# Key words 64 bytes further on, another order of score groups, and two of head 0's steps on VectorE, in a sparse and sliding attention block

## The chip, the cores and the metric

The kernel runs on one core of one Trainium2 chip. The metric is the device time of one execution in microseconds (us), the median of several runs. The profile is of one further execution, taken by the hardware profiler.

## What is computed

One decoder block for 512 tokens of 2048 features, all in float32: a normalisation, a wide projection, two groups of attention heads, a gate on each head, the output projection, the residual sum and a last normalisation. The heads that the change touches are the eight of group A (128 features each, two key groups of four heads):

```python
h = _rmsnorm(x, norm_g[l])
proj = h @ w_in[l]
...
qa = _rope(_heads(qa, N_HEADS_A, HEAD_DIM_A)).reshape(B, S, N_KV_A, GROUP_A, HEAD_DIM_A)
kc = _compress(_rope(_heads(kca, N_KV_A, HEAD_DIM_A)), cmp_k_pos[l], cmp_k_w1[l], cmp_k_w2[l])
...
o_cmp, p_cmp = _compressed_attention(qa, kc, vc)
sel_idx = _select_blocks(p_cmp, S)
o_sel = _selected_attention(qa, _rope(_heads(ksa, N_KV_A, HEAD_DIM_A)), _heads(vsa, N_KV_A, HEAD_DIM_A), sel_idx)
o_win = _banded_attention(qa, _rope(_heads(kwa, N_KV_A, HEAD_DIM_A)), _heads(vwa, N_KV_A, HEAD_DIM_A), WIN_A)
...
o_a = gates[..., 0:1] * o_cmp + gates[..., 1:2] * o_sel + gates[..., 2:3] * o_win
y_a = o_a.reshape(B, S, WIDTH_A) * jax.nn.silu(za)
```

With 512 tokens there are 8 blocks to select from and 16 may be taken, and the window is 512, so both `o_sel` and `o_win` are causal attention over all earlier keys, with keys and values of their own. A head of group A is three softmaxes: over 31 compressed keys and over two full sets of keys.

## The kernel before, in words

**Two words for each number.** [...] To keep float32 precision each operand is split into a high word (a rounded copy, made by ScalarE) and a low word (the rest, a subtraction on VectorE), and each product is three matmuls: high by high, low by high, high by low. `mm3` (L118 to L121) does so for the projections. The splits of the weights are L542 (ScalarE, `whi`) and L543 (VectorE, `wlo`).

**Stages.** In order of time: the norm and the first projections, the eight heads of group B with their projections, the keys and values of group A, the eight heads of group A, the output projection. In the stage of group A's heads `pair(h)` projects the query and the gate of head h by `seven`, a scheme of seven half products of 24 matmuls each, 256 columns wide (named "22", "p", "21", "12", "u", "w", "q" after their operands, written to the banks `pj`). The query comes out in the tile `t` (the buffer "t1", of which there is one: the next head's query can't be begun, L608, before the last reader of this one's is done). `q_done` then rotates it: `turn` (L658 to L666) makes two products with the sine on VectorE (L661) and one with the cosine (L662), and adds them (L664); `q_split` (L257 to L262) makes the high word `qh` on ScalarE (L260) and the low word `ql` by a subtraction (L261). For heads 0 to 5 the sum L664 and the subtraction L261 are on GpSimd, for heads 6 and 7 on VectorE. After the last half product VectorE scales the gate (L677), and ScalarE (L681) and VectorE (L682) make its silu.

**The scores.** `attn_a(h)` takes the four query tiles of 128 tokens in two pairs. The keys lie in two tiles, `KH` (high words) and `KL` (low words), 32 compressed keys first and then 1024 columns in which the two full sets alternate by 128. They are filled for the first key group from L885 on and in `key_words` (L755 on), and after head 3 again, by DMA, with the second group's words (L1027): it is the same two tiles for all eight heads. The score matmuls (L932) put a query tile against the part of the keys that it can see, in groups of columns, each group in one bank of PSUM: one of 288 columns for query tile 0; 288 and 256 for tile 1; 288 and 512 for tile 2; 288, 512 and 256 for tile 3. Every group is done for the three word pairs (`qh` with `KH`, `qh` with `KL`, `ql` with `KH`), so a head has 24 score matmuls and the stage 192. VectorE then takes the minimum with the mask (L934, L938), ScalarE the exponentials (L944, L948) and the scaling (L959), TensorE transposes (L969, L981, L983), and the values follow (L975 to L977, L990, L992).

**What sets the order.** The program is written head after head, but a scheduler puts the instructions of each engine in a fixed order of its own, by a simulated timeline, before anything runs. It mixes the next head's half products between the scores, transposes and value products of the present one. Each engine then works through its list strictly in order. A change of one instruction's engine or shape can so move many others.

**Places of the operands.** The kernel gives its tiles places in steps of 64 bytes: `MOVING, EVEN, STILL, BELOW = 0, 16, 32, 48` are places of weight words in units of 4 bytes, and some tiles are longer than their use (`K` has 32 spare columns). In the program's memory map `KH` and `KL` begin 64 bytes past a multiple of 128 bytes, as `xh` does, whose columns move through TensorE in the half products; `qh` and `ql`, and the weight words that stand still in the half products of this stage, begin at a multiple of 128.

Of the kernel before, what the change touches and what calls it, by code (L numbers as in the profile page):

```python
# [11 lines left out]
F32R = mybir.dt.float32r  # L12
# [5 lines left out]
P = 128  # L18
# [9 lines left out]
CMP = 32  # L28
# [7 lines left out]
def hybrid_block(ctx, tc, xT, xtm, w0, wv0, wv1, wz, wq, wo0, wos, cw1, cw2, cpos, e2, rope, tabs, sinks, gT, fg, out):  # L36
    nc = tc.nc
    pe, act, dve, pool = nc.tensor, nc.scalar, nc.vector, nc.gpsimd

    def sb(name, bufs=1, side=None):  # L40
        return tc.tile_pool(name=name, bufs=bufs, side=side)
# [215 lines left out]
    def q_split(t1, engine=pool):  # L257
        qh = wk.tile([P, S], F32R, name="qh", tag="qh", bufs=1)
        ql = wk.tile([P, S], F32R, name="ql", tag="ql", bufs=1)
        last["qh"] = act.activation(qh, t1, AF.Copy).ins  # L260
        engine.tensor_tensor(out=ql, in0=t1, in1=qh.bitcast(F32), op=ALU.subtract)  # L261
        return qh, ql  # L262
# [231 lines left out]
    kv = kvstack.enter_context(sb("kvA", side="right"))  # L494
# [5 lines left out]
    KH = KL = None  # L500
# [157 lines left out]
    def turn(v, out=None, engine=None):  # L658
        t2 = wk.tile([P, S], F32, name="t2", tag="t2", bufs=1)
        for a, b in ((0, 64), (64, 0)):  # L660
            dve.tensor_tensor(out=t2[a:a + 64], in0=v[b:b + 64], in1=sinA[b:b + 64], op=ALU.mult)  # L661
        dve.tensor_tensor(out=v, in0=v, in1=cosA, op=ALU.mult)  # L662
        if out is None:
            last["turn"] = (engine or dve).tensor_tensor(out=v, in0=v, in1=t2, op=ALU.add).ins  # L664
        else:
            dve.tensor_tensor(out=out, in0=by_block(v), in1=by_block(t2), op=ALU.add)  # L666

    def by_block(v):
        return v.rearrange("p (b j) -> p j b", j=16)

    def pair(h, hooks=None, extra=None):
        def q_done(qv):
            turn(qv, engine=pool if h < 6 else dve)
            return q_split(qv, pool if h < 6 else dve)

        qq, zr = seven(2 + h, done=q_done, hooks=hooks, extra=extra, final=h == 7)
        last["jj"] = dve.tensor_tensor(out=zr, in0=zr, in1=rstdb, op=ALU.mult).ins  # L677

        def silu():
            st = wk.tile([P, S], F32, name="st", tag="st")  # L680
            act.activation(st, zr, AF.Tanh, scale=0.5)  # L681
            dve.scalar_tensor_tensor(out=st, in0=st, scalar=1.0, in1=zr, op0=ALU.add, op1=ALU.mult)  # L682
            return st

        return qq, silu if h == 7 else silu()
# [198 lines left out]
                     "12": [lambda: compressed_values(*hidden)]}, early)  # L884
    ahead.close()  # L885
    kv = kvstack.enter_context(sb("kvK", side="right"))
    KH, KL = [kv.tile([P, CMP + 1056], F32R, name=f"K{e}")[:, 0:CMP + 1024] for e in "HL"]
    for e, k in enumerate((KH, KL)):
        act.activation(k[:, 0:CMP], k0w[:, e].bitcast(F32), AF.Copy)
    sum_of_head = fifth(0)  # L890
# [18 lines left out]
    def attn_a(h, qh, ql, st):  # L909
# [4 lines left out]
        for pair in range(2):  # L914
# [5 lines left out]
            for i in range(2):  # L920
                qt = 2 * pair + i
                n = (qt + 1) * P
                sp = pss.tile([P, 1536], F32, name="sp", tag="sp")
                groups = [(224, 512, 0)]
                if qt >= 1:
                    groups.append((512, 768 if qt == 1 else 1024, 288))
                if qt == 3:
                    groups.append((1024, 1280, 800))
                qs = slice(qt * P, (qt + 1) * P)
                for pi, (qq, kk) in enumerate(((qh, KH), (qh, KL), (ql, KH))):  # L930
                    for (a, b, ko) in groups:
                        pe.matmul(sp[:, a:b], qq[:, qs], kk[:, ko:ko + b - a], start=pi == 0, stop=pi == 2)  # L932
                blk = sp[:, 256:256 + 2 * n].rearrange("p (t w c) -> p w t c", w=2, c=P)
                dve.tensor_tensor_reduce(out=tc_[:, qt, :], in0=sp[:, 224:256], in1=cmask[:, qt * CMP:(qt + 1) * CMP],  # L934
                                         scale=-SCALE_A, scalar=1e38, op0=ALU.add, op1=ALU.min, accum_out=mn[:, i, 0:1])
                for w in range(2):
                    tv = tt[:, off:off + n]
                    last["score", qt] = dve.tensor_tensor_reduce(  # L938
                        out=tv.rearrange("p (t c) -> p t c", c=P), in0=blk[:, w],
                        in1=dmask[:, 512 - n:512].rearrange("p (t c) -> p t c", c=P),  # L940
                        scale=-SCALE_A, scalar=1e38, op0=ALU.add, op1=ALU.min, accum_out=mn[:, i, 1 + w:2 + w]).ins
                    views.append((i, w, tv))
                    off += n
                act.activation(tc_[:, qt, :], tc_[:, qt, :], AF.Exp, bias=mn[:, i, 0:1], scale=-1.0,  # L944
                               accum_out=dn[:, i, 0:1])
                for w in range(2):
                    tv = views[2 * i + w][2]
                    last["exp", qt] = act.activation(tv, tv, AF.Exp, bias=mn[:, i, 1 + w:2 + w], scale=-1.0,  # L948
                                                     accum_out=dn[:, i, 1 + w:2 + w]).ins
# [58 lines left out]
    for h in range(8):  # L1008
        qq, st = pair(h) if h else head0
        if h == 7:  # L1010
            def behind(f, *a):
                with tc.issue_after(last["dma"]):
                    return f(*a)

            first_units = [load_raw(wo0[:, 0, 0])]
            behind(words_back, range(4))
            first_units.append(behind(load_raw, wo0[:, 0, 1]))
            for j in range(4, 8):
                y_back(j)
            behind(words_back, range(4, 6))  # L1020
            first_units.append(behind(load_raw, wo0[:, 0, 2]))
            for j in range(4):
                behind(y_back, j)
        attn_a(h, *qq, st)
        if h == 3:
            for e in range(2):
                nc.sync.dma_start((KH, KL)[e].bitcast(F32), Kd[e])  # L1027
            for kt in range(NQ - 1):
                for e in range(2):
                    nc.sync.dma_start((VH, VL)[e][:, kt].bitcast(F32), Vd[e, :, kt])  # L1030
# [120 lines left out]
    for c, u, ms in ((0, 0, ()), (0, 1, ()), (0, 2, ()), (1, 0, (0, 1, 2)), (1, 1, (3, 4)), (1, 2, (5, 6)), (0, 3, ()),  # L1151
# [4 lines left out]
        with tc.issue_after(recent["mm"]) if (c, u) == (1, 3) else nullcontext():  # L1156
            for j in range(4):
                f = ORDER[4 * u + j]
# [361 lines left out]
```

## Time and profile before

| | us |
|---|---|
| median of 3 runs | 804.39 |
| lowest and highest run | 802.62, 804.96 |
| the profiled execution's own time | 802.8 |
| its span in the profile | 801.0 |

The span is the time from the first to the last instruction; 1.8 us of the profiled execution's time lie outside it. In the profile PE is TensorE (PEld its weight loads), DVE VectorE, ACT ScalarE, POOL GpSimd and SP the queue that issues most DMAs. Consecutive matmuls overlap in the records: each is shown with about 0.28 us, but the next one begins after 0.11 us, so what a matmul costs is read from start to start and not from its own duration. The same holds in part for the other engines, whose next instruction begins a little before the end of the last. The granted clock of TensorE was 0.997 of full speed over the execution. The stage of group A's heads is the stretch from 416 us to 650 us.

### The profile page before, as it was taken

Reading aid. Unit: us, or ns where it says so; the run is one execution under the profiler, and the core shown is the slowest. Engines: PE = TensorE matmul, PEld = TensorE weight load, DVE = VectorE, ACT = ScalarE, POOL = GpSimd, SP = SyncE. Lnnn points to the kernel's source line nnn. Section 1 sums busy time; section 2 is a strip of 40 time slices with the busy share of each in tenths; the row PEclk is TensorE's granted clock in tenths of the full one; section 3 lists DMA queues with packets and bytes.
Section 4 is the critical chain, followed back from the end, with each engine's and each line's share of the span. In section 5 each row is a group of like instructions: output and inputs, shape, how many; then the busy total and the mean of one; then the engine's idle time right before and its main releaser. Section 6 shows DMA issues by size and latency. Waiting matters only on the chain.

```text
span 801.0 us, 15316 instructions
## 1 busy us (share of the span) xinstructions
PE 789.6 (99%) x5693; PEld 739.1 (92%) x5693; DVE 686.3 (86%) x1407; ACT 504.7 (63%) x1103; POOL 108.3 (14%) x111
## 2 busy tenths in 40 slices
PE   9999999999999999999999999999999999999996
PEld 8788888888888899999999999999999999999996
DVE  7668988889989597759999999998999798978895
ACT  6646657655666356664447778777777867553545
POOL 3615002110121000323210110110100000000000
PEclk9999999999999999999999999999999999999998
DMA  7572243564373469887723213225216836797845
GB/s 239 172 242 81 79 144 106 171 171 150 101 210 106 158 200 281 257 269 194 207 82 106 68 53 119 82 92 159 71 50 216 296 120 219 257 266 193 258 86 211
DMA packets 49563, 131.05 MB, mean 164 GB/s; under 512 B 6000, under 2 KB 8848, under 8 KB 49488
## 3 DMA queue, kind: packets, MB, share of 16 engines
q1 hardware_dynamic: 43376, 110.89, 42.3%
q0 software_dynamic: 5824, 18.65, 10.5%
q8 instruction: 45, 0.74, 0.4%
q10 hardware_dynamic: 288, 0.52, 0.2%
q14 instruction: 30, 0.25, 0.1%
HBM read 113.23 MB, written 16.81 MB: 162 GB/s over the span
## 4 chain that ended last, share of the span: by engine, by line
PE 86%; DVE 6%; DMA 3%; ACT 2%; issue 2%; POOL 0%; SPq 0%; DVEq 0%; ACTq 0%
PE pj L119 16%; PE pj L121 15%; PE pj L120 15%; PE oa L120 5%; PE oa L119 5%; PE oa L121 5%; PE sp L932 4%; PE bank L121 2%; PE bank L120 2%; PE bank L119 2%; DMA xr<-xT 2%; DVE wlo L543 2%; PE tp L969 2%; PE tp L384 2%; DMA raw<-wq 1%
## 5 line engine op out<-in xcount | busy, mean ns | idle before, releaser
L119 PE MATMUL pj<-xh,whi 128*128 128x256 f32 (+1 forms) x592 | 196.9, 333 | 0.6 <-ACT t L608 0.5
L121 PE MATMUL pj<-xh,wlo 128*128 128x256 f32 (+1 forms) x592 | 196.2, 331 | 0.0
L120 PE MATMUL pj<-xl,whi 128*128 128x256 f32 (+1 forms) x592 | 196.1, 331 | 0.0
L119 PEld LDWEIGHTS pj<-xh,whi 128*128 128x128 f32 x592 | 111.4, 188 | 11.0 <-ACT t L608 0.9
L121 PEld LDWEIGHTS pj<-xh,wlo 128*128 128x128 f32 x592 | 111.4, 188 | 10.1
L120 PEld LDWEIGHTS pj<-xl,whi 128*128 128x128 f32 x592 | 111.4, 188 | 9.7
L543 DVE TENSOR_TENSOR wlo<-raw,whi 128x1024 fp32r<-128x1024 f32 (+2 forms) x80 | 92.9, 1172 | 7.8 <-ACT whi L542 7.2
L542 ACT ACTIVATE whi<-raw 128x1024 fp32r<-128x1024 f32 (+2 forms) x80 | 77.6, 985 | 30.7 <-DVE raw L581 11.5
L99 DVE TENSOR_TENSOR wlo<-raw,whi 128x1024 fp32r<-128x1024 f32 (+1 forms) x61 | 72.1, 1184 | 22.8 <-ACT whi L97 22.3
L97 ACT ACTIVATE whi<-raw 128x1024 fp32r<-128x1024 f32 (+1 forms) x60 | 56.6, 945 | 28.8 <-PE pj L120 14.8
L120 PE MATMUL oa<-wlo,xh 128*128 128x256 f32 x200 | 55.5, 278 | 0.0
L119 PE MATMUL oa<-whi,xh 128*128 128x256 f32 x200 | 55.4, 278 | 0.0
L121 PE MATMUL oa<-whi,xl 128*128 128x256 f32 x200 | 55.2, 276 | 0.0
L121 PE MATMUL pj<-pu,wlo 128*128 128x256 f32 x160 | 45.0, 281 | 0.5 <-DVE wlo L543 0.5
L119 PE MATMUL pj<-pu,whi 128*128 128x256 f32 x160 | 45.1, 282 | 0.4 <-DVE zr L581 0.4
L120 PE MATMUL pj<-pu,whi 128*128 128x256 f32 x160 | 44.7, 279 | 0.0
L289 DVE TENSOR_TENSOR pl<-tp,ph 128x512 fp32r<-128x512 f32 (+1 forms) x64 | 40.7, 651 | 3.1 <-ACT ph L288 2.9
L288 ACT ACTIVATE ph<-tp 128x512 fp32r<-128x512 f32 (+1 forms) x64 | 34.1, 560 | 9.6 <-PE tp L969 4.4
L363 ACT ACTIVATE ttb<-ttb,sums 128x256 f32<-128x256 f32 (+1 forms) x64 | 30.0, 471 | 14.4 <-DVE sums L356 14.4
L121 PEld LDWEIGHTS oa<-whi,xl 128*128 128x128 f32 x200 | 37.6, 188 | 0.0
L120 PEld LDWEIGHTS oa<-wlo,xh 128*128 128x128 f32 x200 | 37.6, 188 | 0.0
L119 PEld LDWEIGHTS oa<-whi,xh 128*128 128x128 f32 x200 | 37.5, 188 | 0.0
(401 smaller groups left out, 2369.8 us busy)
## 6 DMA issues: line engine op xcount, KB each, us to landing
raw<-wq SPq DMA_DIRECT2D x41, 512.0 KB, 4.4
raw<-wz SPq DMA_DIRECT2D x36, 512.0 KB, 4.0
cw<-cw SPq DMA_DIRECT2D x32, 256.0 KB, 4.0
raw<-wos SPq DMA_DIRECT2D x14, 512.0 KB, 5.9
rw<-wos SPq DMA_DIRECT2D x10, 512.0 KB, 4.8
xr<-xT SPq DMA_DIRECT2D x16, 256.0 KB, 3.4
rows<-xT SPq DMA_DIRECT2D x8, 512.0 KB, 4.7
raw<-wo SPq DMA_DIRECT2D x8, 512.0 KB, 6.0
```

The lines of the kernel that those rows point to most:

```text
L97: last["hi"] = act.activation(hi[:, :width], rw[:, :width], AF.Copy).ins
L99: last["lo"] = dve.tensor_tensor(out=lo[:, :width], in0=rw[:, :width], in1=hi[:, :width].bitcast(F32), op=ALU.subtract).ins
L119: pe.matmul(ps, ah, bh, start=first, stop=False, skip_group_check=go_on)
L120: pe.matmul(ps, ah, bl, start=False, stop=False, skip_group_check=go_on)
L121: recent["mm"] = pe.matmul(ps, al, bh, start=False, stop=last, skip_group_check=go_on).ins
L288: act.activation(ph, tp, AF.Copy)
L289: dve.tensor_tensor(out=pl, in0=tp, in1=ph.bitcast(F32), op=ALU.subtract)
L363: act.activation(tv, tv, AF.Exp, bias=mn[:, e, v:v + 1], scale=-1.0, accum_out=dn[:, e, v:v + 1])
L384: pe.transpose(tp[:, o:o + P], tts[kt + s][:, v, c0:c0 + P], ident)
L542: split_hi = act.activation(hi, src, AF.Copy).ins
L543: last["lo"] = dve.tensor_tensor(out=lo, in0=src, in1=hi.bitcast(F32), op=ALU.subtract).ins
L932: pe.matmul(sp[:, a:b], qq[:, qs], kk[:, ko:ko + b - a], start=pi == 0, stop=pi == 2)
```

## The change

Three edits. The two key tiles begin 16 columns (64 bytes) further on inside their buffers, which have the room, so nothing else moves in memory; both key groups lie in them. In query tile 3 of every head the group of 256 columns comes second and the group of 512 last. For head 0 the sum L664 and the subtraction L261 are on VectorE, as they were for heads 6 and 7; the sum of heads 1 to 5 stays on GpSimd.

```diff
     def pair(h, hooks=None, extra=None):
         def q_done(qv):
-            turn(qv, engine=pool if h < 6 else dve)
-            return q_split(qv, pool if h < 6 else dve)
+            turn(qv, engine=pool if 0 < h < 6 else dve)
+            return q_split(qv, pool if 0 < h < 6 else dve)
...
-    KH, KL = [kv.tile([P, CMP + 1056], F32R, name=f"K{e}")[:, 0:CMP + 1024] for e in "HL"]
+    KH, KL = [kv.tile([P, CMP + 1056], F32R, name=f"K{e}")[:, 16:CMP + 1040] for e in "HL"]
...
                 if qt == 3:
-                    groups.append((1024, 1280, 800))
+                    groups.insert(1, (1024, 1280, 800))
```

The scheduler's order of the instructions changes with it. VectorE's list at the end of head 0's projection, before against now; `t_4493` is head 0's query, `zr` its gate, and `raw` the weights of head 1:

```order
 L581 TENSOR_TENSOR zr<-zr,pj 128x256
 L543 TENSOR_TENSOR wlo<-raw,whi 128x1024
+L664 TENSOR_TENSOR t_4493<-t_4493,t_4689 128x512
 L677 TENSOR_TENSOR zr<-zr,rstdb 128x512
 L581 TENSOR_TENSOR raw<-raw 128x1024
+L261 TENSOR_TENSOR ql<-t_4493,qh 128x512
 L682 SCALAR_TENSOR_TENSOR st<-st,zr 128x512
 L581 TENSOR_TENSOR raw<-raw 128x1024
```

The sum and the low words, which GpSimd did beside this list, now stand in it: the sum behind a weight split, the low words behind the scaling of the gate and a sum of weights. GpSimd has nothing left to do in head 0. ScalarE's list at this place stays as it was: L260, L681, L608.

TensorE's list at query tile 3 of head 0, before against now:

```order
+L119 MATMUL pj<-xh,whi 128x256
+L120 MATMUL pj<-xl,whi 128x256
+L121 MATMUL pj<-xh,wlo 128x256
 L932 MATMUL sp<-KH,qh 128x288
+L932 MATMUL sp<-KH,qh 128x256
 L932 MATMUL sp<-KH,qh 128x512
-L932 MATMUL sp<-KH,qh 128x256
 L932 MATMUL sp<-KL,qh 128x288
+L932 MATMUL sp<-KL,qh 128x256
 L932 MATMUL sp<-KL,qh 128x512
-L932 MATMUL sp<-KL,qh 128x256
```

The nine score matmuls now end with one of 512 columns, and the tile comes three half-product matmuls later. From here to the end of the stage the lists differ in many places: which half-product matmuls stand between which scores, transposes and value products.

## The prediction on record

> **What bounds the kernel now.** I read the page first, then who TensorE waited for, then the stage of group A's heads (416 to 650 us) instruction by instruction. The page's busy times, then the waits of TensorE:
>
> ```profile
> PE 789.6 (99%) x5693; PEld 739.1 (92%) x5693; DVE 686.3 (86%) x1407; ACT 504.7 (63%) x1103; POOL 108.3 (14%) x111
> ...
> PE 86%; DVE 6%; DMA 3%; ACT 2%; issue 2%; POOL 0%; SPq 0%; DVEq 0%; ACTq 0%
> ```
>
> ```profile
> PE bank L176 <- DVE still L173: 1.2, 1, 1.2
> ...
> PE pj L119 <- ACT t L608: 0.5, 1, 0.5
> ...
> PE sp L932 <- DVE sums L938: 0.2, 1, 0.2
> ```
>
> TensorE sets the time: it is busy 99% of the span and makes 86% of the chain that ended last. In the stage of the heads the view of waits names two, 0.5 and 0.2 us. So there are two ways to gain here: to remove such a wait, or to bring the matmuls closer together.
>
> The change touches both. First the wait of 0.5 us, which lies at the end of head 0's projection. The engines' timelines there, GpSimd, VectorE, ScalarE, TensorE (start, duration, engine, line; in brackets the idle time and what ended it):
>
> ```profile
> 416.61 1.28 POOL L664 TENSOR_TENSOR t<-t,t 128x512 f32<-128x512 f32 x1 [21.54 <-DVE t L662]
> 418.64 1.49 POOL L261 TENSOR_TENSOR ql<-t,qh 128x512 fp32r<-128x512 f32 x1 [0.75 <-ACT qh L260]
> ```
>
> ```profile
> 414.63 1.23 DVE L543 TENSOR_TENSOR wlo<-raw,whi 128x1024 fp32r<-128x1024 f32 x1
> 415.77 0.69 DVE L662 TENSOR_TENSOR t<-t,cosA 128x512 f32<-128x512 f32 x1
> 416.37 0.42 DVE L581 TENSOR_TENSOR zr<-zr,pj 128x256 f32<-128x256 f32 x1
> 416.70 2.27 DVE L543 TENSOR_TENSOR wlo<-raw,whi 128x1024 fp32r<-128x1024 f32 x1
> 418.90 1.78 DVE L677 TENSOR_TENSOR zr<-zr,rstdb 128x512 f32<-128x512 f32 x1
> 420.60 1.21 DVE L581 TENSOR_TENSOR raw<-raw 128x1024 f32<-128x1024 f32 x1
> 421.73 0.68 DVE L682 SCALAR_TENSOR_TENSOR st<-st,zr 128x512 f32<-128x512 f32 x1
> ```
>
> ```profile
> 417.93 0.64 ACT L260 ACTIVATE qh<-t 128x512 fp32r<-128x512 f32 x1 [1.63 <-POOL t L664]
> 420.71 0.63 ACT L681 ACTIVATE st<-zr 128x512 f32<-128x512 f32 x1 [2.15 <-DVE zr L677]
> 421.25 0.36 ACT L608 ACTIVATE t<-pj 128x256 f32<-128x256 f32 x1
> ```
>
> ```profile
> 420.47 0.28 PE L121 MATMUL pj<-pu,wlo 128*128 128x256 f32 x1
> 420.59 0.29 PE L932 MATMUL sp<-KH,qh 128*128 128x288 f32 x1
> 420.71 0.30 PE L932 MATMUL sp<-KL,qh 128*128 128x288 f32 x1
> 420.85 0.29 PE L932 MATMUL sp<-KH,ql 128*128 128x288 f32 x1
> 421.66 0.39 PE L119 MATMUL pj<-xh,whi 128*128 128x256 f32 x1 [0.52 <-ACT t L608]
> 421.88 0.28 PE L120 MATMUL pj<-xl,whi 128*128 128x256 f32 x1
> ```
>
> While GpSimd runs, VectorE's split takes 2.27 us against 1.23 for the same shape just before, and its scaling L677 takes 1.78 against 0.69 for another product of that shape (L662). VectorE so comes 2.1 us late, ScalarE waits 2.15 us for L677, its copy L608 runs at 421.25, and TensorE, which wants to go on at about 420.98 (0.13 after its third score matmul), begins at 421.66: 0.7 us lost.
>
> Second, the pace of the matmuls. Stretches of half products, first and last start, from the timeline of TensorE:
>
> ```profile
> 415.83 0.28 PE L119 MATMUL pj<-xh,whi 128*128 128x256 f32 x1
> ...
> 424.71 0.28 PE L120 MATMUL pj<-xl,whi 128*128 128x256 f32 x1
> ...
> 428.22 0.52 PE L932 MATMUL sp<-KH,qh 128*128 128x288 f32 x2
> ...
> 429.30 0.28 PE L119 MATMUL pj<-pu,whi 128*128 128x256 f32 x1
> ...
> 434.29 0.28 PE L121 MATMUL pj<-xh,wlo 128*128 128x256 f32 x1
> 434.40 0.64 PE L932 MATMUL sp<-KH,qh 128*128 128x288 f32 x3
> ...
> 435.84 0.28 PE L119 MATMUL pj<-xh,whi 128*128 128x256 f32 x1
> ...
> 437.95 0.28 PE L119 MATMUL pj<-qw,whi 128*128 128x256 f32 x1
> ```
>
> From 415.83 to 420.47 lie 41 steps, 113 ns each. From 421.88 to 424.71, right behind query tile 0's scores, 24 steps take 118 ns each, with the same engine clock and shape. From 429.30 to 434.29, behind tile 2's scores (which end with 512 columns), 44 steps take 113 ns again; from 435.84 to 437.95, behind tile 3's nine (which end with 256), 18 steps take 117 ns. So TensorE has two paces, 4.6 ns apart, it keeps one for a whole stretch, and the scores between switch it. What switches it the trace doesn't say; that operands' places have a part in it is a surmise from the fact that engine, shape and clock are the same.
>
> **The change part by part.** *Head 0 on VectorE.* Removed from GpSimd: 1.28 and 1.49 us; added to VectorE, priced by the two heads where it does them now:
>
> ```profile
> L261 DVE TENSOR_TENSOR ql<-t,qh 128x512 fp32r<-128x512 f32 x2 | 1.4, 688 | 0.0
> ...
> L664 DVE TENSOR_TENSOR t<-t,t 128x512 f32<-128x512 f32 x2 | 1.4, 684 | 0.0
> ```
>
> 0.69 us each, about 0.60 from start to start (L662 to the next). With GpSimd silent I lay VectorE's new list out with its undisturbed steps: split 416.70, next start 1.14 later (as from 414.63 to 415.77), sum L664 at 417.84, scaling L677 at 418.44, weights L581 at 419.04, low words L261 at 420.18, done at 420.9. ScalarE: `qh` at 418.55, silu L681 at 419.2, both early. But L608 overwrites head 0's query, which L261 still reads. The view of tile `ql` lists ScalarE's L608 among those who waited for it:
>
> ```profile
> ACT t L608: 4.6, 4
> ```
>
> So L608 starts at about 420.95 instead of 421.25 and ends at 421.3; TensorE goes on at 421.35 instead of 421.66. The third score, at 420.85, needs `ql` too and comes some 0.1 us later, inside the same wait. Gain 0.3 us, not 0.7: the weights' sum L581, 1.2 us in front of L261, eats the rest. Bounds: 0.7 if it slides behind or the copy isn't held, nothing if the first weights arrive later than I think. Behind it stand L682 and a second L581; they start some 0.8 us earlier than before, which nobody on TensorE is shown to want.
>
> *The score matmuls themselves.* The view by source line counts them:
>
> ```profile
> L932 PE MATMUL sp<-KH,qh x64: 276/296/398, 420.6 to 637.1; 128*128 128x288 f32 x32, 128*128 128x256 f32 x16, 128*128 128x512 f32 x16
> ```
>
> 64 of each of three word pairs, 192. No run shows the new place of the keys under these operands. The nearest price is the difference of the two paces: 4.6 ns x 192 = 0.9 us, a gain or a loss. The nearest row for operands that both begin at the same place in 128 bytes is in an earlier stage (there 64 bytes past it, both), 512 columns:
>
> ```profile
> 77.24 0.39 PE L119 MATMUL opb<-xh,whi 128*128 128x512 f32 x1
> ...
> 80.64 0.39 PE L119 MATMUL opb<-xh,whi 128*128 128x512 f32 x1
> ```
>
> 15 steps, 226.7 ns each. The tile that starts at 428.22 (above) has three pairs of 288 and 512 columns in 1.08 us (to 429.30), 360 a pair; with 227 for the wide one, 133 are left for 288 columns, more than the 127.5 that 113.3 x 288/256 gives. I take a gain of 0.3 us.
>
> *Tile 3's new order.* It now ends with 512 columns, as tile 2 does, behind which the trace shows the quick pace. The slow stretch behind tile 3 costs 18 x 4 ns = 0.08 us; eight heads, 0.6 us. I take 0.5, since the key words moved as well and tile 2's pattern may not hold; bounds 0.6 and 0.
>
> *The stretches behind the other 24 tiles* change by the keys' place and by the new mixture. A stretch like that behind tile 0 (24 steps) costs 24 x 4.6 = 0.11 us when it is slow. If half are slow now, the two ends are 1.3 us of gain and of loss. I take a gain of 0.2: the place now equals that of `qh` and `ql`, as in the quick stage above, but the half products around keep theirs.
>
> The scheduler's other moves I cost at nothing: TensorE's list is full, and DVE's added 1.4 us lie in a stage where it has
>
> ```profile
> 416.00:650.00 234.00, 233.27 (x1959) 230.47 (x1959) 217.37 (x476) 180.36 (x446) 19.07 (x12) 1.00 0.36 119
> ```
>
> 16.6 of 234 us free (third busy time) and take 2.1 us of blocking away. If that cover fails, a late weight split costs TensorE about the 0.2 to 0.5 us of the two waits above, so 1 us either way goes into the range.
>
> Sum: 0.3 + 0.3 + 0.5 + 0.2 = 1.3 us of gain. Against the profiled execution's own time, 802.8 us, that gives 801.5. This execution stands 1.6 us under the median of the runs, 804.39; carried over, 803.1. About 0.3% (2.4 us) is what a measurement of this kernel can tell from no change: faster means under 802.0, slower over 806.8.
>
> **The rivals.** *The quick pace wins almost everywhere.* The scores gain 0.8, tile 3's stretches 0.6, the others 1.3, the wait goes whole, 0.7: together 3.4 us, 801.0. For it: 113 ns is the pace of most stretches above, and one switch sets a whole stretch. Against it: slow stretches begin after tile 0's scores too, where no order changes.
>
> *The place of the key words has no effect.* Then tile 3's order has none either, since there is no reason left why its end should matter, and only the 0.3 us at head 0 stay: 804.1. For it: that the two paces come from places is surmise. Against it: the pace follows what stood before, with all else equal. [...]
>
> *The slow pace wins: slower.* The new place makes the scores leave TensorE at 118 ns. Price: 0.9 us in the scores, less 0.3 at head 0, and 4.6 ns for every half-product matmul that turns from quick to slow. The same stage's row for the half products alone counts them:
>
> ```profile
> 416.00:650.00 234.00, 169.32 (x1314) 159.05 (x1313) 12.50 (x30) 7.83 (x21) 1.00 0.36 119
> ```
>
> 1314. From 390 of them on (1.8 us) it is over 0.3%; half of them, 657, cost 3.0 us, with the rest 3.6: 808.0. For it: behind tile 3, the state already lasted until the transposes. Against it: it must hit three in ten of all, and the end with 512 columns speaks for the other pace.
>
> *The edits don't do what they say:* the queue order shows both moved steps, and the new place holds for all heads, so this has no chance of its own.
>
> **How the numbers follow.** Forecast as summed 0.48 (its own range 801.3 to 805.0), quick pace 0.28, no effect of places 0.12, slow pace 0.12. Faster by over 0.3%: the quick pace and 0.05 of the forecast's edge, 0.33. Slower: 0.12. Within: 0.43 + 0.12 = 0.55. The range goes from 800.2 (the quick pace with most of the 1 us of the scheduler) to 805.8 (no effect, with the same the other way), and leaves out most of the slow case and the tails, about 0.2.
>
> **What the profile of the changed kernel would show.** No GpSimd work in head 0; VectorE's split at 1.23 us and L677 at 0.69 there; L608 right behind L261; the wait of TensorE for L608 at 0.2 us or gone. Behind tile 3's scores 113 ns from start to start in most heads. Pairs of 288 and 512 columns under 0.36 us. Wrong would be: `pj` stretches at 118 ns behind most tiles, a wait of TensorE for `wlo` or `ql` that isn't there now, or a stage whose length differs from 234 us by another amount than these terms.

## The result and the profile after

| | kernel before | changed kernel |
|---|---|---|
| median of the runs, us | 804.38 (802.62 to 804.96, 4 runs) | 813.23 (811.47 to 814.65, 4 runs) |
| ratio, with its 95% interval | | 1.0113 (1.0086 to 1.0139) |
| the profiled execution, us | 802.8 | 814.65 |
| its span, us | 801.0 | 812.9 |

The change makes the kernel 8.9 us slower; the interval of the ratio says 7 to 11 us. The forecast of 803.1 and its range up to 805.8 are both missed. The page of the changed kernel, busy times and chain:

```profile
PE 795.9 (98%) x5693; PEld 742.6 (91%) x5693; DVE 685.8 (84%) x1409; ACT 504.6 (62%) x1103; POOL 105.5 (13%) x109
...
PE 71%; DVE 13%; ACT 6%; DMA 6%; issue 3%; SPq 0%; POOL 0%; ACTq 0%; DVEq 0%
```

VectorE works no longer than before. TensorE's busy time grows by 6.3 us for the same 5693 matmuls: each is shown with about 0.28 us while the next begins after 0.11, so a delay shorter than the difference counts as busy. The chain moves as well. TensorE makes 71% of it and no longer 86%; VectorE has 13% and not 6%, ScalarE 6% and not 2%, DMA 6% and not 3%. The end is now set by handovers between engines. Who TensorE waited for (sum in us, times, longest):

```profile
PE pj L121 <- DVE wlo L543: 2.0, 5, 0.8
PE pj L119 <- ACT whi L542: 1.6, 2, 0.8
...
PE pj L119 <- ACT xh L1047: 1.1, 1, 1.1
PE sp L932 <- DVE sums L938: 1.0, 2, 0.8
PE oa L120 <- DVE wlo L1052: 0.7, 1, 0.7
...
PE sp L932 <- POOL ql L261: 0.3, 1, 0.3
...
PE op L976 <- DVE pl L289: 0.2, 1, 0.2
```

These seven rows are 6.9 us. Of these 4.4 lie in the heads' stage, where the view of before had 0.7, and 1.8 behind it. The other 0.7 lie ahead of it: of the five waits for L543 only two, 1.3 us, are in the stage; three are earlier, where the kernel before has two as well, of 0.5 us. None of the rows is at head 0. In the stage they are weight splits (L542, L543), softmax sums (L938) and low words (L261 on GpSimd, for head 1, and L289); behind the heads, the splits of the output projection (L1047, L1052). The stage of the heads in one row, to be held against the one the prediction quotes:

```profile
416.00:650.00 234.00, 229.44 (x1886) 224.74 (x1885) 206.75 (x457) 172.18 (x428) 16.14 (x10) 0.99 0.34 113
```

TensorE did 1886 matmuls until 650 us and not 1959, and VectorE, which was given work, was busy 206.75 us and not 217.37. Nobody is overloaded: all do less in the same time, because they wait for each other.

To see where time is lost I counted, for two traces, when TensorE had begun the same number of columns; the difference is the lag of the one behind the other. The lag of the changed kernel behind the kernel before, by the time of the latter:

| at, us | 400 | 430 | 450 | 500 | 520 | 580 | 600 | 640 | 650 | 680 | 700 |
|---|---|---|---|---|---|---|---|---|---|---|---|
| lag, us | -0.1 | -0.4 | 0.7 | 1.4 | 3.3 | 3.3 | 6.6 | 8.0 | 8.1 | 10.3 | 11.5 |

At head 0 the changed kernel is ahead. Then it falls back in steps near 446, 455, 516, 600, 638, 680 and 694 us of its own time, and from 700 us on nothing changes. The step at 516 us on ScalarE, VectorE and TensorE:

```profile
509.32 0.71 ACT L948 ACTIVATE tt<-tt,sums 128x512 f32<-128x512 f32 x1
509.93 0.19 ACT L948 ACTIVATION_READ_ACCUMULATOR tt<-tt,sums 128x1 f32 x1
513.10 0.69 ACT L957 ACTIVATE pc<-tc__5546,sums 128x128 f32<-128x128 f32 x2 [2.98 <-DVE sums L952]
513.70 2.34 ACT L959 ACTIVATE tt<-tt,sums 128x384 f32<-128x384 f32 x4
515.94 0.36 ACT L619 ACTIVATE zr<-pj 128x256 f32<-128x256 f32 x1
516.20 1.99 ACT L542 ACTIVATE whi<-raw 128x1024 fp32r<-128x1024 f32 x2
```

```profile
509.14 1.23 DVE L543 TENSOR_TENSOR wlo<-raw,whi 128x1024 fp32r<-128x1024 f32 x1
510.40 0.42 DVE L581 TENSOR_TENSOR t<-t,pj 128x256 f32<-128x256 f32 x1
510.74 0.69 DVE L682 SCALAR_TENSOR_TENSOR st<-st,zr 128x512 f32<-128x512 f32 x1
511.34 1.22 DVE L581 TENSOR_TENSOR raw<-raw 128x1024 f32<-128x1024 f32 x1
512.48 0.16 DVE L950 TENSOR_SCALAR sums<-sums 128x6 f32<-128x6 f32 x1
...
512.89 0.17 DVE L952 TENSOR_TENSOR sums<-sums,gates 128x6 f32<-128x6 f32 x1
```

```profile
517.30 0.38 PE L119 MATMUL pj<-pu,whi 128*128 128x256 f32 x1 [0.78 <-ACT whi L542]
```

ScalarE is done with the exponentials at 510.1 us and then stands still for 2.98 us: the next step in its list, L957, needs the normalisers L950 to L952, and VectorE's list has four larger steps in front of these. The copy L619 and the weight split L542 stand behind L957 and L959. By the program the copy has to wait for L682, which reads the gate that it overwrites (until 511.43 us), and for the half product that it copies (its last matmul is shown from 511.33 to 511.61 us), and the split for the weights that L581 makes (until 512.56 us). So for the last 1.5 us of the idle time the copy could run, and the split, which begins at 516.20, comes 3.6 us after its weights are there; TensorE waits for it. ScalarE takes its list strictly in order here: 1.5 us idle with a step ready behind the waiting one.

The largest step, 3.5 us near 600 us, has two parts. TensorE's waits there, and then two stretches of the view by windows (TensorE's granted clock is the third number from the end):

```profile
600.81 0.38 PE L119 MATMUL pj<-xh,whi 128*128 128x256 f32 x1 [0.79 <-ACT whi L542]
...
602.07 0.45 PE L121 MATMUL pj<-xh,wlo 128*128 128x256 f32 x1 [0.76 <-DVE wlo L543]
```

```profile
602.00:605.60 3.60, 3.53 (x17) 3.53 (x18) 1.68 (x8) 3.60 (x11) 0.00 (x0) 0.53 0.02 5
605.80:612.00 6.20, 6.20 (x50) 5.95 (x49) 4.77 (x13) 4.14 (x12) 0.00 (x0) 1.00 0.02 6
```

Two waits for splits stand close together, and right behind them the granted clock is about half for 3.4 us: 16 steps take 213 ns each and not 113, which is 1.6 us. In e2 (below), which is as slow, the clock is 1.00 over the whole stage, and behind a wait of 0.76 us for the same split the steps take 120 ns, so the slow clock adds to the loss of this execution and isn't what makes it. The profiled execution, 814.65 us, is the slowest of the four; whether the others have this stretch isn't known.

### The profile page after: what moved, and what is told of

It is laid out like the page before. It is cut to its first block, busy times and chain, and to the rows that moved or that the text cites. A ratio compares the mean times of both kernels' runs of the same rounds, so it can differ in the third digit from the quotient of the medians.

```text
span 812.9 us, 15329 instructions
## 1 busy us (share of the span) xinstructions
PE 795.9 (98%) x5693; PEld 742.6 (91%) x5693; DVE 685.8 (84%) x1409; ACT 504.6 (62%) x1103; POOL 105.5 (13%) x109
## 3 DMA queue, kind: packets, MB, share of 16 engines
q0 software_dynamic: 5824, 18.65, 10.6%
## 4 chain that ended last, share of the span: by engine, by line
PE 71%; DVE 13%; ACT 6%; DMA 6%; issue 3%; SPq 0%; POOL 0%; ACTq 0%; DVEq 0%
PE pj L121 13%; PE pj L119 13%; PE pj L120 13%; PE oa L120 4%; PE oa L121 4%; PE oa L119 4%; DVE wlo L543 4%; PE bank L121 2%; PE bank L120 2%; PE bank L119 2%; DMA xr<-xT 2%; PE sp L932 2%; DVE raw L581 2%; PE tp L384 2%; ACT whi L542 1%
## 5 line engine op out<-in xcount | busy, mean ns | idle before, releaser
L543 DVE TENSOR_TENSOR wlo<-raw,whi 128x1024 fp32r<-128x1024 f32 (+2 forms) x80 | 91.0, 1150 | 11.0 <-ACT whi L542 9.4
L542 ACT ACTIVATE whi<-raw 128x1024 fp32r<-128x1024 f32 (+2 forms) x80 | 77.3, 983 | 24.7 <-DVE raw L581 9.3
L289 DVE TENSOR_TENSOR pl<-tp,ph 128x512 fp32r<-128x512 f32 (+1 forms) x64 | 40.6, 650 | 3.0 <-ACT ph L288 2.8
```

The source lines that it names most:

```text
L289: dve.tensor_tensor(out=pl, in0=tp, in1=ph.bitcast(F32), op=ALU.subtract)
L542: split_hi = act.activation(hi, src, AF.Copy).ins
L543: last["lo"] = dve.tensor_tensor(out=lo, in0=src, in1=hi.bitcast(F32), op=ALU.subtract).ins
```

## The experiments

The theories named in the first four expectations: A, the scheduler's new lists of the engines cost the time; B, the new place of the key words brings the slow pace of the matmuls; C, the two steps on VectorE cost it themselves. All ratios are against runs of the kernel before, measured beside them on the same chip.

To hold lists, some kernels tie each instruction to the one ahead of it in a given list of its engine, without any semaphore, ahead of the scheduling:

```diff
         hybrid_block(tc, *args, out)
+        _keep_lists(tc, nc)
...
+            if before is not None:
+                tc.add_manual_dep(i, before.name, info, reason="list")
```

### Which part costs the time

**e1: the words alone.** Only this edit; the scheduler writes the same lists as before.

```diff
-    KH, KL = [kv.tile([P, CMP + 1056], F32R, name=f"K{e}")[:, 0:CMP + 1024] for e in "HL"]
+    KH, KL = [kv.tile([P, CMP + 1056], F32R, name=f"K{e}")[:, 16:CMP + 1040] for e in "HL"]
```

> Only the key words begin 64 bytes further on; every engine's list stays that of before. Theory A (the new lists of the engines cost the time): 803 to 805 us, at most 1.5 us off before, since 192 score matmuls at 4.6 ns are 0.9 us. Theory B (the new place puts TensorE in the slow pace): 807 to 813. Theory C (the two steps cost time by being on VectorE): 803 to 805.

803.59 us, ratio 1.0002 (0.9988 to 1.0016). Tile 2 of head 0 and the matmul behind it in this trace:

```profile
428.59 0.52 PE L932 MATMUL sp<-KH,qh 128*128 128x288 f32 x2
...
429.68 0.28 PE L119 MATMUL pj<-pu,whi 128*128 128x256 f32 x1
```

Three pairs of 288 and 512 columns take 1.09 us, 363 ns each; they took 360 before. The place of the keys doesn't change the time, and B falls.

It does change the pace of some stretches, both ways. Behind tile 3 of head 0, 18 steps of half products take 113 ns each here, and behind that of head 1, 13 steps; the scores have their old order, and the kernel before takes 117 and 118 there. The stage has 55 stretches of eight or more half products that can be compared in six traces. In nine of them the three traces with the old place (before, e3, e7) agree on the pace, the three with the new place (e1, e5, e6) agree too, and the two differ: six stretches, 131 steps, turn quick, and three, 59 steps, turn slow. At 4 to 5 ns a step, the net is an estimated 0.3 us.

**e2: head 0 on VectorE alone**, with the lists that the scheduler then makes.

```diff
-            turn(qv, engine=pool if h < 6 else dve)
-            return q_split(qv, pool if h < 6 else dve)
+            turn(qv, engine=pool if 0 < h < 6 else dve)
+            return q_split(qv, pool if 0 < h < 6 else dve)
```

> Only head 0's sum and low words go to VectorE, with the lists that the scheduler then makes; the scores and key words stay. Theory A (lists): 810 to 815 us, nearly all of the loss. Theory B (place of the words): 803 to 805. Theory C (the work on VectorE itself): 810 to 815.

813.44 us, ratio 1.0129 (1.0105 to 1.0154): the whole loss of the change. It is in this edit or in what the scheduler makes of it.

**e3: the same edit, the lists of the kernel before held**, the two steps put where the scheduler has them on VectorE.

> Head 0's sum and low words on VectorE, but every engine's list pinned to that of before; the two instructions stand in VectorE's list where the changed kernel has them, behind the weight split and behind the first sum of weights. Theory A (lists): 803 to 805 us, 0.3 under before by the sum made for head 0. Theory B (place): 803 to 805. Theory C (the work on VectorE itself): 810 to 815.

802.81 us, ratio 0.9988 (0.9977 to 0.9999): 1.0 us faster than before, and not slower. (The same program, measured again as e7, gives 0.9996.) Head 0 on VectorE, ScalarE and TensorE:

```profile
417.79 0.68 DVE L664 TENSOR_TENSOR t<-t,t 128x512 f32<-128x512 f32 x1
418.39 0.68 DVE L677 TENSOR_TENSOR zr<-zr,rstdb 128x512 f32<-128x512 f32 x1
418.99 1.22 DVE L581 TENSOR_TENSOR raw<-raw 128x1024 f32<-128x1024 f32 x1
420.12 0.68 DVE L261 TENSOR_TENSOR ql<-t,qh 128x512 fp32r<-128x512 f32 x1
```

```profile
420.90 0.38 ACT L608 ACTIVATE t<-pj 128x256 f32<-128x256 f32 x1 [1.16 <-DVE ql L261]
```

```profile
421.34 0.39 PE L119 MATMUL pj<-xh,whi 128*128 128x256 f32 x1
```

This is the layout of the prediction to within 0.06 us at each step. C falls.

**e4: GpSimd as before, but the lists of e2 held** for all other instructions.

> The code of before with both steps on GpSimd, but every engine's list pinned to the one that the scheduler made for head 0 on VectorE (the lists of e2_dve). Theory A (lists): 810 to 815 us, as slow as e2_dve though nothing moved to VectorE. Theory B (place): 803 to 805. Theory C (the work on VectorE itself): 803 to 805.

813.26 us, ratio 1.0117 (1.0098 to 1.0135). Without any of the three edits the new lists alone cost 9.5 us. A holds: two steps of 0.7 us moved, and the lists that the scheduler wrote around them cost all of it.

**e5: all three edits, the lists of before held**, and **e6**, the same with the low words ahead of the sum of weights in VectorE's list:

```diff
 L664 t<-t,t
 L677 zr<-zr,rstdb
+L261 ql<-t,qh
 L581 raw<-raw
-L261 ql<-t,qh
```

> All three edits (key words 64 bytes on, tile 3's groups in the new order, head 0's sum and low words on VectorE), with each engine's list of the kernel before held; the two moved steps stand on VectorE where the changed kernel has them, and only the groups of tile 3 change places. Theory A (the new lists of the engines cost the time): about 802.3 us, against 803.8 for the kernel before: the 1.0 us that head 0 alone gave with the old lists, and 0.5 for tile 3. Rival B' (the two placement edits cost something once they stand together, which neither the words alone nor VectorE alone showed): 804 or more. Either way no wait of TensorE for whi or wlo in the heads' stage.

> As e5, and one step more: on VectorE head 0's low words L261 stand ahead of the weights' sum L581 (1.2 us) instead of behind it. If the prediction's reading is right that this sum eats the rest of head 0's wait, L608 starts as soon as its product is there, at about 420.8 us, and TensorE goes on at 421.2 or before, 0.15 us or more sooner than in e3 (421.34). If the sum's lateness is what counts instead (the weights L581 feed a split that TensorE needs next), TensorE goes on no sooner, or loses about 0.5 us at the next weights. In the total the difference to e5 is under 0.5 us and inside the interval: the trace decides.

e5: 802.1 us, ratio 0.9985 (0.9972 to 0.9998); e6: 802.15 us, 0.9983 (0.9968 to 0.9998). Both beat the kernel before, e5 by 1.2 us with an interval from 0.2 to 2.2, and the changed kernel by some 10 us (1.0113 less 0.9985 of 803.3). The stage of the heads in e5, and the nine scores of tile 3 of head 1 with the half products behind them:

```profile
416.00:650.00 234.00, 233.79 (x1968) 231.32 (x1967) 217.09 (x480) 180.72 (x447) 16.32 (x10) 1.00 0.36 119
```

```profile
462.34 0.63 PE L932 MATMUL sp<-KH,ql 128*128 128x288 f32 x3
462.81 0.28 PE L120 MATMUL pj<-xl,whi 128*128 128x256 f32 x1
...
464.29 0.28 PE L121 MATMUL pj<-xh,wlo 128*128 128x256 f32 x1
```

1968 matmuls until 650 us. Behind tile 3, which now ends with 512 columns, 13 steps take 113.8 ns each, where before they took 118. But e1 takes 113 here with the scores in their old order: what goes with the quick pace at this place is the new place of the words, and not the order. Behind tile 3 of head 5 it goes with the order: 118 ns in before, e3, e7 and e1, 113 in e5 and e6. In e6 TensorE goes on 0.13 us after the third score, so without a wait, but it does so in e5 too, where VectorE happened to run 0.4 us further ahead of TensorE than in e3. That the sum of weights is what holds the rest of head 0's wait is therefore not shown; one execution's lead of VectorE is worth as much. e7, whose program is that of e3, goes on 0.14 us after its third score, and e3 0.48.

### Are other lists better

**e10: only the sum L664 on VectorE; e11: only the low words L261.** Each with the lists that the scheduler makes for it.

```diff
-            turn(qv, engine=pool if h < 6 else dve)
+            turn(qv, engine=pool if 0 < h < 6 else dve)
```

```diff
-            return q_split(qv, pool if h < 6 else dve)
+            return q_split(qv, pool if 0 < h < 6 else dve)
```

> Only head 0's sum of rotation products L664 on VectorE, the low words L261 still on GpSimd; the engines' lists as the scheduler draws them for this program. Theory S (any move between engines makes the scheduler draw other lists for the heads' stage, and their quality is a matter of luck): slower by some us or not, between 801 and 815, with waits of TensorE for whi or wlo wherever it is slower. Rival (it is the low words' move that spoils the lists): 803 to 804.

> Only head 0's low words L261 on VectorE, the sum L664 still on GpSimd; lists as drawn for this program. Theory S: anything between 801 and 815, with waits of TensorE for whi or wlo where it is slower. Rival (the sum's move spoils the lists): 803 to 804.

808.78 us, ratio 1.0055 (1.0033 to 1.0078), and 810.32 us, 1.0082 (1.0059 to 1.0105). Either move makes other lists for the whole stage, and both are slower, with TensorE's wait for L543 on top of the view, 1.5 us and here 2.1 us (e11), 1.2 and 2.0 of it in the heads' stage:

```profile
PE pj L121 <- DVE wlo L543: 2.1, 5, 0.8
```

So neither move is the guilty one. Counting the changed kernel and e2, four sets of lists that the scheduler wrote anew cost 4 to 11 us more than those of the kernel before. Four relatives are no proof of a rule; no set better than the old one was seen.

### Where in the program

The lists of before (with head 0 on VectorE) and those of e2 hold the same steps ahead of the first score of head 0, so one can be followed up to there and the other from there on. **e7** was to have the new lists up to that place; **e8** has them up to the first projection matmul behind the heads (there the sets differ by five instructions), **e12** up to the first score of head 3 (they differ by eight), and each has the old lists behind it. In the lists of an engine:

```diff
-old[0 : end]
+new[0 : cut]
+old[cut : end]
```

> Head 0 on VectorE; every engine keeps the new lists (those of e2) until the first score matmul of the heads' stage, and the lists of before from there on (both lists hold the same steps ahead of that place, so the cut is clean). Theory A1 (the cost falls place by place, where the new order leaves TensorE waiting, and adds up): the lag of e2 behind e3 at that place was 1.6 us, so about 804.4 us. Rival A2 (the cost is made in the heads' stage alone, the earlier lag is given back there): 802.8 us. Rival A3 (the early lists set what comes behind): 808 or more.

> As e7, but the new lists are kept until the first projection matmul behind the heads (642 us in e2), the lists of before from there on. Theory A1: the lag of e2 behind e3 there was 7.6 us, and the 3.8 us behind it go away, so about 810.3 us. Rival A2' (what is behind the heads is late only as a consequence, and comes in any case): 813.4 us. Rival (the lists of before win some of the lag back): 806 to 809 us.

> Head 0 on VectorE; the new lists (those of e2) until the first score matmul of head 3 (510.8 us in e2), the lists of before from there on. Theory P (in the heads' stage the cost falls place by place and is kept): e8 was 1.8 us further behind e7 there than at the stage's beginning, so about 804.6 us. Rival (it is given back by the lists of before, which leave room): 802.8. Rival (the order of the first heads sets the later waits): 808 or more.

e7: 802.78 us, ratio 0.9996 (0.9983 to 1.001). But e7 is no test of lists: up to that place the two sets hold the same steps in the same order, so its kernel is that of e3, letter for letter. It is a second measurement of e3, and between A1, A2 and A3 it doesn't decide. It shows two things. The gain of e3 over before, 1.0 us there, comes out as 0.3 us here (from -0.8 to 1.4). And the 1.6 us of lag that I had read in e2 at 416 us belonged to that one execution, since the lists up to there are the same in e2, e3 and e7.

e8: 814.91 us, ratio 1.0135 (1.0114 to 1.0157). With the old lists behind the heads the total doesn't fall. In the trace the steps at 680 and 694 us are gone, but at the seam stands one wait instead:

```profile
645.18 0.39 PE L975 MATMUL op<-ph,VH 128*128 128x256 f32 x1 [2.64 <-ACT ph L288]
```

```profile
646.40:649.70 3.30, 3.30 (x15) 3.11 (x15) 2.37 (x3) 2.00 (x5) 0.00 (x0) 0.50 0.00 1
```

The last head's softmax is late by then, and the next step in TensorE's list, the value product L975, waits for it; the projection matmul behind it starts at 645.40 us. Behind the wait the granted clock is at half for the 3.3 us of the second row, as in the changed kernel near 602 us, which costs 1.6 us more. I had expected 810.3. The total is that of A2', but a seam is neither list's own, and what it adds, 4.2 us, is about what the old lists were to win; so e8 doesn't decide between A1 and A2'.

e12: 807.09 us, ratio 1.0041 (1.0027 to 1.0054), 2.5 us above what I expected. At 500 us it lies 1.6 us behind e3, as theory P says; near the seam it loses 2.3 us more, of which the view shows one wait of 0.94 us, for the scaling L959; from there to the end the lag stays at 3.9 us. With the old lists from head 3 on none of the waits appears that e2 has at the later heads, nor those at 680 and 694 us. So the loss is made place by place and is not given back. In the changed kernel 8.1 of 11.5 us of lag are made by 650 us; whether the rest, behind the heads, comes of the lists there or follows from the stage isn't shown.

### What in the lists

**e9: three weight splits earlier** in the lists of e2; near 517 us VectorE's sum of weights L581 also goes ahead of L682. ScalarE's list near 517 us, as an example:

```diff
+L619 zr<-pj
+L542 whi<-raw
 L957 pc<-tc,sums
...
 L959 tt<-tt,sums
-L619 zr<-pj
-L542 whi<-raw
```

> The lists of e2 (head 0 on VectorE, 813.4 us), with three weight splits put earlier in ScalarE's list, at the three places where TensorE waits most directly for one: at 455 and 485 us the copy L619 and the split L542 behind it go ahead of the last softmax steps L959 that stand before them, at 517 us ahead of L957, and there VectorE's weight sum L581 goes ahead of L682. Theory M (TensorE waits because the split stands late in an in-order list, and what is won there is kept): the waits at those places (0.74, 0.32 and 0.98 us) go, about 811.4 us. Rival G (the softmax steps that now stand behind the split are late instead, or the next place waits longer): the three waits go, but the total stays at 813.

813.38 us, ratio 1.0114 (1.0093 to 1.0135). The three waits for splits are gone. At 517 us another stands in their place:

```profile
514.60 0.68 ACT L957 ACTIVATE pc<-tc__5546,sums 128x128 f32<-128x128 f32 x2
...
515.18 2.34 ACT L959 ACTIVATE tt<-tt,sums 128x384 f32<-128x384 f32 x4
```

```profile
515.83 0.44 PE L969 MATMUL tp<-ident,tt 128*128 128x128 f32 x2 [0.68 <-ACT tt L959]
```

The transposes now wait for the softmax that the split was put ahead of, and near 637 us the wait for L938 grows from 0.5 to 1.1 us. Against e2 the lag falls by 1.7 us from 430 to 520 us, 1.2 are left of it at the end, and the medians of the runs (813.38 and 813.44) show nothing of that. The run doesn't decide between M and G: part of what is won is given back, and it is too little for the interval.

**e13: the normalisers first.** L950, L951 and L952 of five query tiles go ahead of the weight steps on VectorE (of two tiles L951 and L952 only, since L950 stood there already); **e14** moves two splits as in e9 as well. VectorE's list near 514 us:

```diff
 L543 wlo<-raw,whi
 L581 t<-t,pj
+L950 sums<-sums
+L951 sums<-sums
+L952 sums<-sums,gates
 L682 st<-st,zr
 L581 raw<-raw
-L950 sums<-sums
-L951 sums<-sums
-L952 sums<-sums,gates
```

> The lists of e2 (head 0 on VectorE, 813.4 us), with the small steps L950, L951, L952 of five query tiles (near 446, 478, 495, 514 and 572 us) put on VectorE right behind the softmax step that they need, ahead of the weight sums and splits that stood before them. Theory N (ScalarE stands idle for L952 and everything behind it in its list is late: softmax steps, weight splits, then TensorE): ScalarE's waits for L952, 10.0 us in e2, fall under 4, TensorE's waits at 455, 485 and 517 us go, and about 2 us or more are won and kept: 811.4 or less. Rival G (what is won is given back at the next place, since TensorE's own list is what is short of work there): total 813, with other waits in the view.

> As e13, and ScalarE's copy L619 and split L542 at 455 and 485 us ahead of the softmax steps that stand before them. Theory N: as e13 or up to 0.5 us less, since the splits were late for the normalisers' sake. If the splits' own place counts apart from that: 1 us less than e13. Rival G: 813.

e13: 810.39 us, ratio 1.0079 (1.006 to 1.0099), 3.0 us under e2 by the medians and 4.0 by the ratios (the two were measured on different chips), with intervals that don't meet. e14: 810.07 us, 1.0078 (1.0054 to 1.0101), the same. ScalarE's waits for the normalisers, of before, of e2 and of e13:

```profile
ACT pc L957 <- DVE sums L952: 2.2, 2, 1.9
```

```profile
ACT pc L957 <- DVE sums L952: 10.0, 5, 3.4
```

```profile
ACT pc L957 <- DVE sums L952: 0.7, 1, 0.7
```

The place shown above for the changed kernel, in e13, ScalarE and TensorE:

```profile
510.13 0.69 ACT L957 ACTIVATE pc<-tc__5546,sums 128x128 f32<-128x128 f32 x2 [0.67 <-DVE sums L952]
...
513.24 2.00 ACT L542 ACTIVATE whi<-raw 128x1024 fp32r<-128x1024 f32 x2
```

```profile
515.45 0.36 PE L119 MATMUL pj<-pu,whi 128*128 128x256 f32 x1
```

No wait for a split is left at 455, 485 and 517 us, though the one for L289 at 447 us grows from 0.2 to 1.2 us. Against e2 the lag falls by 2.4 us from 430 to 520 us, and 2.1 of it are left at the end: won and mostly kept. Theory N holds for these places, and the splits' own place adds nothing to it (e14). It explains some 2 to 4 of the 10.6 us.

The lists of before don't have these normalisers earlier. In e5 L952 of this same tile comes 7 us after the last exponential that it rests on, yet TensorE doesn't wait:

```profile
504.31 0.15 DVE L952 TENSOR_TENSOR sums<-sums,gates 128x6 f32<-128x6 f32 x1
```

```profile
504.43 1.06 ACT L542 ACTIVATE whi<-raw 128x1024 fp32r<-128x1024 f32 x1 [0.23 <-DVE raw L581]
505.39 0.68 ACT L957 ACTIVATE pc<-tc__5546,sums 128x128 f32<-128x128 f32 x2
```

There ScalarE's list has the split ahead of L957, and TensorE's list has other work until then. So a late step costs nothing where the lists of the three engines agree on what comes late; that this is what makes the whole list good is argued from this place and not shown.

Open is most of what is left in e13, 7.6 us against e3: the view of TensorE's waits has 1.2 us at 447 us and 3.5 us at 600, 635, 678 and 692 us, and the rest lies in gaps too small for it. For the later places e12 shows that the loss goes with the lists from head 3 on, but which steps there are in the wrong order was not tried. Nor is it shown why one moved step makes the scheduler order work differently 200 us later.

## Why the prediction was wrong

**The step that failed** is the one on the scheduler: its other moves cost nothing, with 16.6 us of free time on VectorE as the cover and "1 us either way" in the range. They cost 10.6 us (e2 against e3, medians measured side by side) or 10.3 us (the changed kernel against e5, by their ratios). Both halves of the argument were wrong. The cover was an average over 234 us, and VectorE's free time even grew, to 27.3 us; a list in strict order loses time at its head and not for lack of room (2.98 us on ScalarE in front of L957, with the copy ready for the last 1.5). And the price was taken from the two waits that the trace of before had. Those are the waits of lists that fit each other; they bound nothing for lists that don't. The order of the program, shown with the change, said that the lists differ in many places from tile 3 of head 0 to the stage's end, and I gave this no rival. What would have shown it in advance is which step heads ScalarE's list when VectorE's is late: normalisers, then softmax, then the split that TensorE needs.

**Head 0** was right: each step within 0.06 us in e3, TensorE at 421.34 us against 421.35. Its gain was put at 0.3 us; e3's ratio gives 1.0 us (0.1 to 1.8), that of the same program in e7 0.3 us (-0.8 to 1.4), and the lag of e3 behind before falls by 0.4 us there, of which 0.1 is left at the end of the trace. That the sum of weights holds the rest isn't shown (e5, e6, e7).

**The score matmuls themselves** were put at 0.3 us of gain; e1 gives no change, within 1.3 us, and 363 ns a pair against 360. The estimate had drawn on a stage with other matmuls.

**Tile 3's order** came out as forecast in e5 and e6, the quick pace behind the tile, but for the most part not for the reason given: at heads 0 and 1 the new place of the words alone brings it (e1), and only at head 5 does it go with the order. The 0.5 us were too much as well: the sum took all eight heads to be slow, while in the kernel before only three of the seven stretches of eight or more steps behind tile 3 are, 44 steps, 0.2 us. In the total it can't be told from the interval; between 430 and 650 us e5 wins 0.7 us on e3, of two executions.

**The other stretches** were put at 0.2 us. The place does move some of them, to the quick pace and to the slow (e1); the net can't be told from nothing in the time.

The four terms make 1.3 us, and e5, which is the change without the new lists, wins 1.2 us (0.2 to 2.2). That the two agree so well is luck: the interval is wider than the sum, and of the four terms only that of head 0 is seen at about its size in a trace. Of the rivals, "the place has no effect" was right on the time of the words (e1) and wrong on the pace; "slow pace wins" named a slower kernel for a cause that didn't come. The sign named as the prediction's failure, a wait for `wlo` or `ql` that wasn't there before, is the one that came: for `wlo` twice in the heads' stage, 1.3 us, and for `ql` once, 0.3 us.

## What to carry to other kernels

Where a scheduler writes each engine's list, moving even a small step can mean testing other lists, whose effect is many times that of the step (here 10 us for two steps of 0.7 us): hold the old lists and make the edit alone, and only then judge it. A free share of an engine is no cover in a strict order (here 16.6 of 234 us on VectorE, and some 10 us lost); look for the step at the head of a list that waits while a step that the busiest engine needs stands ready behind it. When a wait is removed and another takes its place, go up the chain to the first late step, here three operations on 6 columns.

## What the hardware showed besides

TensorE showed two paces here, 113 and 118 ns for the same matmul at a granted clock of 1.00 over the heads' stage. The place of the keys changes which of them some stretches have (e1), at head 5 it goes with the scores' order (e5, e6), and the same program has other paces in another execution: e3 and e7 differ in 7 of the 55 stretches. What sets the pace is open.

The granted clock fell to half twice in these traces' heads: for 3.4 us behind two waits of 0.79 and 0.76 us that were 0.5 us apart (the changed kernel), and for at least 3.3 us behind one of 2.64 us (e8). Behind a single wait of 1.06 us, at 681.8 us in the changed kernel, it was 1.00 (676 to 690 us).

A step on 6 columns took as long as one on 1024 while GpSimd was at work. In e2, at head 1, L950 takes 1.25 us and not 0.17 as at 514.10 us, and the sum of weights L581 right in front of it 1.21:

```profile
446.10 1.25 DVE L950 TENSOR_SCALAR sums<-sums 128x6 f32<-128x6 f32 x1
```

```profile
445.24 2.08 POOL L261 TENSOR_TENSOR ql<-t,qh 128x512 fp32r<-128x512 f32 x1 [0.74 <-ACT qh L260]
```

It ends at 447.35 us, 0.03 us after GpSimd's L261, which itself takes 2.08 us there and 1.49 in head 0 of the kernel before. What held the small step isn't shown.
